# Hymba block in three-pass fp32r: PSUM pools by phase (single banks, double banks), and attention emitted in runs of two pairs

## The chip, the cores and the metric

One Trainium2 chip, one of its cores. The metric is the device time of one launch in microseconds. The kernel before takes 2512.08 us, the median of three runs (2510.38 to 2513.5).

## The reference

One decoder layer over x of 2048 tokens by 1024 channels, in float32:

```
hn    = rmsnorm(x, norm_mix_g)
x_lru, g_lru, q, k, v = split(hn @ w_in)          # 1024, 1024, 16x64, 2x64, 2x64
xc    = causal_conv4(x_lru)
r, i  = sigmoid(blockdiag(xc, w_a) + b_a), sigmoid(blockdiag(xc, w_x) + b_x)
a     = exp(-8 * r * softplus(-lam))
h_t   = a_t * h_(t-1) + sqrt(1 - a_t^2) * (i_t * xc_t)      # scan over tokens
y_lru = h * gelu(g_lru)
y_att = sliding window attention (window 128, learned sinks, 16 q heads, 2 kv heads)
x     = x + concat(rmsnorm(y_lru), rmsnorm(y_att)) @ w_out
x     = x + square(relu(rmsnorm(x) @ w_up)) @ w_down
out   = rmsnorm(x, norm_final_g)
```

The second mixer's norm needs the sum of squares of y_lru over all 1024 channels of a token, so it is complete only when the last block of channels is through the scan.

## The kernel before, in words

The 2048 tokens go through in two chunks of 1024 (`c` = 0, 1). Every fp32 product is three matmul passes in fp32r, hi·hi, hi·lo and lo·hi: ScalarE copies the operand to `hi` (L178 for weights), VectorE subtracts to get `lo` (L179).

A chunk has these stages. Stage 1 loads x, norms it (L208) and transposes it on TensorE (`tps`, L218), with the splits behind at L222 to L224. Then come the k and v projections (`kps`, `vps`, opened by `new_kv`, products at L236, L237, L239). The attention loop walks slots `s` = 0 to 16: in slot s, for four pairs `p` of query blocks, it emits `scores(p)` of head s (`sc`, L610), `values` of two older pairs (`av`, L664), `probs(p)` of head s-1 (two transposes `tp`, L640, read by ACT at L643 and DVE at L644 into `pf`), and one `piece`, six matmuls of a projection for later (`qps`, then `xps`, `gpps`). Every second slot ends a projection of q, whose splits `qs` stand at L588 and L589. Two heads of y are transposed by `flip` (`ytp`, L683). The LRU loop follows over eight channel blocks j: projections, convolution (L719), gates (`gps`, L879 to L881), the scan (L892), y (L896), its square (L900) and the sum `accq` (L901; for the last block on POOL). `token_rstd(accq)` transposes that sum (`sqt`, L701) to get the norm `r_lr`. Then W_out: matmuls `ops` (L960), added into x by DVE (L965), first the attention half of the rows (with `r_at`, known since attention's end), then the LRU half (with `r_lr`). The MLP's first half, `Up.run`, runs 16 pairs of hidden blocks, each of seven half-width products of a Strassen scheme (84 matmuls at L410) into `pa`, `pb` and the two halves of one tile `qr`; the DVE additions into `hid` stand at L440, L443 and L448. In its last pair chunk 0 starts stage 1 of chunk 1. The second half of the MLP (`dd`, L1187) runs after both chunks, with PSUM of its own.

What sets the order: the code is emitted in the order above, and a list scheduler of the framework then reorders it for each engine by what is ready, subject to the buffers; on the chip each engine's queue runs in that fixed order. A tile of PSUM can be given out when the last reader of its tag is through. PSUM before is laid out once for all stages but the last: two tiles of two banks (`mm0`, `mm1`) and four single ones (`b01` with two buffers, `b2`, `b3`):

```
    mmp = ps_stack.enter_context(tc.tile_pool(name="mmp", bufs=1, space=PSUM))
    hbp = ps_stack.enter_context(tc.tile_pool(name="hbp", bufs=1, space=PSUM))
```

`sqt` takes `b2` and `b3`; `ops` rotates through `mm0`, `mm1` and `b01`, so the two don't share a bank. In the attention `tp` is one bank with two halves, used by turns: pair p+2 waits until pair p's half was read.

Of the kernel before, what the change touches and what calls it, by code (L numbers as in the profile page):

```python
# [8 lines left out]
F32 = mybir.dt.float32  # L9
# [7 lines left out]
PSUM = bass.MemoryType.PSUM  # L17

P = 128
SEQ = 2048  # L20
D = 1024
# [4 lines left out]
HALF = 512  # L26
# [11 lines left out]
def hybrid_block_kernel(  # L38
# [40 lines left out]
    const = ctx.enter_context(tc.tile_pool(name="const", bufs=1))  # L79
    small = ctx.enter_context(tc.tile_pool(name="small", bufs=4))  # L80
    slots = ctx.enter_context(tc.tile_pool(name="slots", bufs=1))
    ps_stack = ExitStack()
    mmp = ps_stack.enter_context(tc.tile_pool(name="mmp", bufs=1, space=PSUM))
    hbp = ps_stack.enter_context(tc.tile_pool(name="hbp", bufs=1, space=PSUM))

# [21 lines left out]


    def bank(i, name, shape=(P, HALF)):
        if i < 2:
            return hbp.tile(list(shape), F32, name=name, tag="b01", bufs=2)
        return hbp.tile(list(shape), F32, name=name, tag=f"b{i}")

    def pair(i, name):

# [2 lines left out]
    mm_next = [0]  # L120

    def mm(name, i=None):

        if i is None:
            i = mm_next[0]
            mm_next[0] ^= 1
        return mmp.tile([P, D], F32, name=name, tag=f"mm{i}")

    def mm_halves(name, i=None):
        ps = mm(name, i)  # L130
        return [ps[:, :HALF], ps[:, HALF:]]

# [166 lines left out]
    class Up:  # L299
# [117 lines left out]
        def pair(self, fp):  # L417

            pa, pb = bank(fp % 2 * 2, "pa"), bank(fp % 2 * 2 + 1, "pb")
            qr = mm("qr", fp % 2)  # L420
            pq, pr = qr[:, :HALF], qr[:, HALF:]
            lo, hi = slice(0, HALF), slice(HALF, D)
            sc = U((11, 15)[fp % 2], "sc", F32, (P, 2, HALF))
            self.prod(pa, fp, "A11", "B11", True)
            act.activation(sc[:, 0], pa, AF.Copy)
            yield
            self.prod(pb, fp, "A12", "B21", True)
            c1 = self.hidden()
            dve.tensor_tensor(c1[:, lo], pb, sc[:, 0], op=ALU.add)
            yield  # L430
            self.prod(pa, fp, "S2", "T2", False)
            act.activation(sc[:, 1], pa, AF.Copy)
            yield
            self.prod(pq, fp, "A22", "T4", True)
            yield
            self.prod(pa, fp, "S3", "T3", False)
            s3 = small.tile([P, HALF], F32, name="s3", tag="s3", bufs=1)
            act.activation(s3, pa, AF.Copy)
            c2 = self.hidden()
            dve.tensor_tensor(c2[:, lo], pq, s3, op=ALU.add)  # L440
            yield
            self.prod(pr, fp, "S1", "T1", True)
            dve.tensor_tensor(c2[:, hi], pr, s3, op=ALU.add)  # L443
            act.activation(c2, c2, AF.Relu)
            act.activation(c2, c2, AF.Square)
            yield
            self.prod(pr, fp, "S4", "B22", False)
            dve.tensor_tensor(c1[:, hi], pr, sc[:, 1], op=ALU.add)  # L448
            act.activation(c1, c1, AF.Relu)
            act.activation(c1, c1, AF.Square)  # L450
            a12 = U(13, "a12", F32, (P, 2, HALF))
            a4 = U(14, "a4", F32, (P, HALF))
            dve.tensor_tensor(a12[:, 0], c1[:, hi], c2[:, hi], op=ALU.add)
            dve.tensor_tensor(a12[:, 1], a12[:, 0], c1[:, lo], op=ALU.subtract)
            dve.tensor_tensor(c1[:, hi], c1[:, lo], c1[:, hi], op=ALU.subtract)
            dve.tensor_tensor(a4, c2[:, lo], a12[:, 1], op=ALU.subtract)
            g, r = divmod(fp, 2)
            for o, y in enumerate((c1[:, lo], c2[:, hi], a12[:, 1], c2[:, lo], c1[:, hi], a4, a12[:, 0])):
                nc.sync.dma_start(actd[self.c][g][:, :, o, r * 2 * P:(r + 1) * 2 * P],
                                  y.rearrange("p (s n) -> p s n", s=2))  # L460
            yield
# [32 lines left out]
            self.next = (hn, steps) if steps else (None, None)  # L494

    def new_kv():
        k = mm("kps", 1)
        return k, ((k[:, :HALF], k[:, HALF:]), pair(0, "vps"))

# [10 lines left out]
    for c in range(NCH):  # L510
# [83 lines left out]
        class Head:  # L594
# [38 lines left out]
                dve.tensor_scalar(self.ls, self.ls, PSCALE, None, op0=ALU.mult)  # L633
                dve.reciprocal(self.ls, self.ls)

            def probs(self, p):

                tp = tpb[:, p % 2]
                for i in range(2):
                    pe.transpose(tp[:, i, :], self.st[:, 2 * p + i, :], ident)  # L640
                pf = U((20, 21, 12, 14)[pf_next[0] % 4], "pf", F16, (P, 3, 2, 2, P))
                pf_next[0] += 1
                act.activation(pf[:, 0, 0], tp, AF.Copy, scale=PSCALE)  # L643
                dve.scalar_tensor_tensor(out=pf[:, 0, 1], in0=tp, scalar=PSCALE, in1=pf[:, 0, 0],  # L644
                                         op0=ALU.mult, op1=ALU.subtract)

                nc.gpsimd.affine_select(out=pf[:, 1], in_=pf[:, 0], compare_op=ALU.is_gt, fill=0.0, base=0,  # L647
                                        pattern=[[0, 4], [-1, P]], channel_multiplier=1)
                nc.gpsimd.affine_select(out=pf[:, 2], in_=pf[:, 0], compare_op=ALU.is_ge, fill=0.0, base=0,
                                        pattern=[[0, 4], [1, P]], channel_multiplier=-1)  # L650
                self.pf[p] = pf
# [129 lines left out]
        lru_in = None  # L781
        for s in range(NH + 1):
            j = s // 2
            if s < NH:
                if s % 2 == 0:
                    yqs[j] = U(3 + j % 2, "yq", F32, (P, NT, P))
                heads[s] = Head(s, qs[j][s % 2], yqs[j])
            if s % 2 == 1:
                if j + 2 < KT:
                    piece, done = new_q(j + 2)  # L790
                else:
                    piece, done = (new_x if j + 2 == KT else new_gate)(0)
            for p in range(4):
                if s < NH:
                    heads[s].scores(p)
                    if p == 3:
                        heads[s].sums()
                if len(late) == 4:
                    for _ in range(2):
                        heads[late[0][0]].values(late.pop(0)[1])  # L800
                if s > 0:
                    heads[s - 1].probs(p)
                    late.append((s - 1, p))
                    if p == 3 and s % 2 == 1 and s > 1:
                        flip(j - 1, yqs[j - 1])
                piece(p if s % 2 else 4 + p)
            if s % 2 == 0:
                if j + 1 < KT:
                    qs[j + 1] = done()
                elif j + 1 == KT:  # L810
                    lru_in = done()
                else:
                    lru_in.append(done())
# [109 lines left out]
                parts.append(whole(new_gate(j + 1)))  # L923

        r_lr = token_rstd(accq, "lr")


        x1 = []
# [161 lines left out]
            dn.split("T1")  # L1090

    up.run(ahead)
    ps_stack.close()
    ddp = ctx.enter_context(tc.tile_pool(name="ddp", bufs=4, space=PSUM, reuse_waits="tile"))
    g3 = load_g(g_fin)

# [182 lines left out]
```

## Time and profile before

| what | value |
|---|---|
| median of three runs | 2512.08 us |
| profiled execution | 2512.32 us |
| span of its instructions | 2510.6 us |
| PE busy | 2420.6 us, 96% of the span |
| DVE busy | 1766.3 us, 70% |
| ACT busy | 1254.5 us, 50% |
| POOL busy | 457.4 us, 18% |
| mean granted TensorE clock | 0.996 of full speed |

The profiled execution is 0.24 us above the median of the runs, and 1.72 us of it lie outside the span. Stages in the trace: attention of chunk 0 from 65 to 257 us, LRU to 429, W_out to 617, first half of the MLP to 934; chunk 1 the same with attention from 997 to 1187, LRU to 1360, W_out to 1548, the first half to 1878; the second half to the end. PE is the engine in question: its times here are starts of instructions, since its ends are modelled and run on under the next start.

### The profile page before, as it was taken

How to read it: one execution, taken by the hardware profiler on the slowest of the kernel's cores; microseconds unless marked ns; L12 is line 12 of the kernel's file. 1: busy time of each engine (PE TensorE's matmuls, PEld its weight loads, DVE VectorE, ACT ScalarE, POOL GpSimd, SP SyncE). 2: the span in 40 equal slices, each digit the busy share in tenths (PEclk: the TensorE clock that was granted, in tenths of full speed). 3: DMA queues.
4: the chain of work that ended last, by engine and by line, in shares of the span. 5: the costliest groups of instructions: out<-in, count | busy, mean ns of one | idle time of the engine just before them, and what ended most of it. 6: DMA issues, size and time to landing. Idle time of an engine off the chain costs nothing.

```text
span 2510.6 us, 32534 instructions
## 1 busy us (share of the span) xinstructions
PE 2420.6 (96%) x12338; PEld 1974.2 (79%) x12338; DVE 1766.3 (70%) x2400; ACT 1254.5 (50%) x2084; POOL 457.4 (18%) x455
## 2 busy tenths in 40 slices
PE   7999999999999998999999998999999999999998
PEld 6877787787788877887778787788878877888886
DVE  6887566756655565886667847655564898887889
ACT  6666777414455455666778315444554233322335
POOL 0445000001333210454000001322310110111100
PEclk9999999999999999999999999999999999999999
DMA  4111113312344443111113312344464454443334
GB/s 161 37 52 52 45 46 107 115 51 100 118 142 155 157 155 130 43 52 51 46 45 124 111 42 101 133 145 146 148 212 129 154 163 147 142 138 122 125 98 164
DMA packets 132812, 276.37 MB, mean 110 GB/s; under 512 B 11184, under 2 KB 70576, under 8 KB 132656
## 3 DMA queue, kind: packets, MB, share of 16 engines
q1 hardware_dynamic: 124880, 246.50, 29.4%
q0 software_dynamic: 5184, 18.88, 2.0%
q10 hardware_dynamic: 2592, 8.91, 0.9%
q8 instruction: 97, 1.59, 0.3%
q14 instruction: 59, 0.48, 0.1%
HBM read 190.37 MB, written 83.89 MB: 109 GB/s over the span
## 4 chain that ended last, share of the span: by engine, by line
PE 66%; DVE 15%; issue 9%; ACT 7%; DMA 2%; POOL 1%; POOLq 0%; SPq 0%; ACTq 0%; DVEq 0%
PE dd L1187 14%; PE ops L960 10%; PE qr L410 10%; PE pa L410 9%; PE pb L410 3%; PE sc L610 2%; PE qps L239 2%; PE qps L236 2%; PE qps L237 2%; DVE xc L719 2%; DVE acc L1196 1%; PE xps L237 1%; PE xps L236 1%; PE xps L239 1%; DVE wlo L179 1%
## 5 line engine op out<-in xcount | busy, mean ns | idle before, releaser
L1196 DVE TENSOR_TENSOR acc<-dd,acc 128x1024 f32<-128x1024 f32 x211 | 255.4, 1219 | 85.1 <-PE dd L1187 84.6
L960 PE MATMUL ops<-whi,ht 128*128 128x512 f32 x1024 | 278.4, 391 | 1.0 <-DVE x L965 1.0
L990 ACT ACTIVATE ah<-araw 128x1024 fp32r<-128x1024 f32 x96 | 101.9, 1062 | 293.0 <-PE dd L1187 286.6
L960 PEld LDWEIGHTS ops<-whi,ht 128*128 128x128 f32 x1024 | 192.2, 188 | 42.7 <-DVE x L965 2.5
L960 PE MATMUL ops<-wlo,ht 128*128 128x512 f32 x512 | 159.7, 391 | 0.6 <-DVE wlo L179 0.5
L388 POOL TENSOR_TENSOR s<-wraw 128x512 f32<-128x512 f32 x32 | 43.0, 1343 | 593.2 <-issue 321.0
L178 ACT ACTIVATE whi<-wraw 128x1024 fp32r<-128x1024 f32 x84 | 88.5, 1054 | 120.7 <-PE ops L960 86.2
L647 POOL TENSOR_SCALAR_AFFINE_SELECT pf<-pf 128x512 f16<-128x512 f16 x128 | 87.3, 682 | 333.4 <-DVE pf L644 327.0
L991 DVE TENSOR_TENSOR al<-araw,ah 128x1024 fp32r<-128x1024 f32 x96 | 123.4, 1287 | 11.0 <-ACT ah L990 10.9
L624 ACT ACTIVATE st<-sc,mx 128x128 f32<-128x128 f32 x256 | 91.6, 364 | 60.1 <-DVE mx L621 59.6
L179 DVE TENSOR_TENSOR wlo<-wraw,whi 128x1024 fp32r<-128x1024 f32 x84 | 106.5, 1274 | 20.0 <-ACT whi L178 9.5
L960 PEld LDWEIGHTS ops<-wlo,ht 128*128 128x128 f32 x512 | 95.5, 188 | 21.4 <-DVE wlo L179 2.3
L236 PE MATMUL qps<-ht,whi 128*128 128x512 f32 x256 | 107.8, 421 | 0.0
L396 ACT ACTIVATE f2h<-wraw 128x1024 fp32r<-128x1024 f32 x32 | 33.9, 1061 | 142.6 <-DMA act<-hid 111.9
L237 PE MATMUL qps<-ht,whi 128*128 128x512 f32 x256 | 101.7, 397 | 0.0
L236 PE MATMUL xps<-ht,whi 128*128 128x512 f32 x256 | 101.5, 397 | 0.0
L239 PE MATMUL qps<-ht,wlo 128*128 128x512 f32 x256 | 101.3, 396 | 0.0
L237 PE MATMUL xps<-ht,whi 128*128 128x512 f32 x256 | 101.0, 394 | 0.0
L236 PE MATMUL gpps<-ht,whi 128*128 128x512 f32 x256 | 100.8, 394 | 0.0
L410 PE MATMUL qr<-hm,s 128*128 128x512 f32 x384 | 97.6, 403 | 2.7 <-DVE hid L443 2.7
L237 PE MATMUL gpps<-ht,whi 128*128 128x512 f32 x256 | 100.1, 391 | 0.0
L397 DVE TENSOR_TENSOR f2l<-wraw,f2h 128x1024 fp32r<-128x1024 f32 x32 | 39.1, 1223 | 79.1 <-ACT f2h L396 79.1
(327 smaller groups left out, 6852.5 us busy)
## 6 DMA issues: line engine op xcount, KB each, us to landing
araw<-act SPq DMA_DIRECT2D x96, 512.0 KB, 3.5
wraw<-in_w_up_dram SPq DMA_DIRECT2D x64, 512.0 KB, 3.2
act<-hid SPq DMA_DIRECT2D x128, 256.0 KB, 2.6
wraw<-in_w_in_dram SPq DMA_DIRECT2D x52, 512.0 KB, 3.2
act<-a SPq DMA_DIRECT2D x96, 256.0 KB, 2.6
wraw<-in_w_out_dram SPq DMA_DIRECT2D x32, 512.0 KB, 3.2
braw<-in_w_down_dram SPq DMA_DIRECT2D x28, 512.0 KB, 4.3
xt<-in_x_dram SPq DMA_DIRECT2D x16, 512.0 KB, 4.6
```

The lines of the kernel that those rows point to most:

```text
L178: act.activation(hi, raw, AF.Copy)
L179: (eng or dve).tensor_tensor(lo, raw, f32(hi), op=ALU.subtract)
L236: pe.matmul(ps[m], w[0][:, k * P:(k + 1) * P], hk(ht[m][0], k), start=(k == 0), stop=False)
L237: pe.matmul(ps[m], w[0][:, k * P:(k + 1) * P], hk(ht[m][1], k), start=False, stop=False)
L239: pe.matmul(ps[m], w[1][:, k * P:(k + 1) * P], hk(ht[m][0], k), start=False, stop=(k == KT - 1))
L410: pe.matmul(ps, w[a_][:, ks], hk(h[b_], k), start=first and k == 0 and i == 0, stop=k == KT // 2 - 1 and i == 2, skip_group_check=True)
L624: ins = act.activation(self.st[:, b, :], cur[:, i, :], AF.Exp, bias=self.mx[:, b:b + 1], accum_out=self.ls[:, b:b + 1])
L960: pe.matmul(ps[m], a_, wk[k][b_][:, hs], start=(k == 0 and a_ is yh and b_ == 0), stop=(k == kn - 1 and a_ is ylo))
L990: act.activation(hi, raw, AF.Copy)
L991: dve.tensor_tensor(lo, raw, f32(hi), op=ALU.subtract)
L1187: pe.matmul(o[:, i, :], a_[:, t0:t0 + P], b_[:, r, :], start=first and r == 0 and k == 0, stop=r == 1 and k == 2, skip_group_check=True)
L1196: dve.tensor_tensor(accs[blk][d_], o, accs[blk][d_], op=ALU.add)
```

## The change

Three things. First, `psum(*names)` closes the open pools of PSUM and opens others. A phase "sbp" has eight single banks `s0` to `s7`; it is open at the start (stage 1), and again from behind `r_lr` on: for W_out, the MLP's first half and the next chunk's stage 1. `new_kv` opens the old layout (`doubles()`) for projections, attention and LRU. Second, the tile `qr` of the MLP's first half becomes two tiles of a bank each, `pq` and `pr`; `mm_halves` gives two tiles where "sbp" is open. Third, the attention loop emits two pairs at a time: two `scores`, two `values`, two `probs`, two `piece`s. The odd pair of `probs` writes its transposes into `free`, half of an `mm` tile that no projection uses just then, the even one into `tpb`.

```diff
-    ps_stack = ExitStack()
-    mmp = ps_stack.enter_context(tc.tile_pool(name="mmp", bufs=1, space=PSUM))
-    hbp = ps_stack.enter_context(tc.tile_pool(name="hbp", bufs=1, space=PSUM))
+    phase = [None, {}]
+    def psum(*names):
+        if phase[0]:
+            phase[0].close()
+        phase[:] = [ExitStack(), {}]
+        for name in names:
+            phase[1][name] = phase[0].enter_context(
+                tc.tile_pool(name=name, bufs=1, space=PSUM, reuse_waits="tile"))
+    def doubles():
+        psum("mmp", "hbp")
+    psum("sbp")
...
     def bank(i, name, shape=(P, HALF)):
+        if "sbp" in phase[1]:
+            return half(4 + i, name)
...
+    def half(i, name):
+        return phase[1]["sbp"].tile([P, HALF], F32, name=name, tag=f"s{i}")
...
     def mm_halves(name, i=None):
+        if "sbp" in phase[1]:
+            if i is None:
+                i = mm_next[0]
+                mm_next[0] ^= 1
+            return [half(2 * i, name), half(2 * i + 1, name)]
...
-            qr = mm("qr", fp % 2)
-            pq, pr = qr[:, :HALF], qr[:, HALF:]
+            pq, pr = half(fp % 2 * 2, "pq"), half(fp % 2 * 2 + 1, "pr")
...
     def new_kv():
+        doubles()
...
-            def probs(self, p):
-                tp = tpb[:, p % 2]
+            def probs(self, p, free):
+                if p % 2 and free:
+                    tp = free[p // 2][:, :2 * P].rearrange("p (a n) -> p a n", a=2)
+                else:
+                    tp = tpb[:, p // 2]
...
+            free = mm_halves("tp", (s + 1) // 2 % 2) if 0 < s < NH - 1 else None
...
-            for p in range(4):
+            for p0 in (0, 2):
                 if s < NH:
-                    heads[s].scores(p)
-                    if p == 3:
+                    for p in (p0, p0 + 1):
+                        heads[s].scores(p)
+                    if p0:
                         heads[s].sums()
...
-                    heads[s - 1].probs(p)
-                    late.append((s - 1, p))
-                    if p == 3 and s % 2 == 1 and s > 1:
+                    for p in (p0, p0 + 1):
+                        heads[s - 1].probs(p, free)
+                        late.append((s - 1, p))
+                    if p0 and s % 2 == 1 and s > 1:
                         flip(j - 1, yqs[j - 1])
-                piece(p if s % 2 else 4 + p)
+                for p in (p0, p0 + 1):
+                    piece(p if s % 2 else 4 + p)
...
         r_lr = token_rstd(accq, "lr")
+        psum("sbp")
```

Line numbers move with it: L236, L237, L239 become L258, L259, L261; L410 is L432, L443 is L464, L589 is L611, L610 is L632, L644 is L669, L640 is L665, L701 is L726, L879 to L881 are L910 to L912, L901 is L932, L960 is L992.

How the queues move is shown at three places. The first is PE at the end of the LRU of chunk 0 (`sqt` transposes the sum `accq`, `gps` are the last gates, `ops` W_out's matmuls). Before:

```order
L960 MATMUL ops<-whi,ht 128x512 x4
L960 MATMUL ops<-wlo,ht 128x512 x2
L960 MATMUL ops<-whi,ht 128x512 x4
L960 MATMUL ops<-wlo,ht 128x512 x2
L960 MATMUL ops<-whi,ht 128x512 x2
L960 MATMUL ops<-whi,ht 128x512 [waits DVE_49] x2
L701 MATMUL sqt<-ident,accq 128x128 [waits Pool_49]
L701 MATMUL sqt<-ident,accq 128x128 x3
L701 MATMUL sqt<-ident,accq 128x128 [waits Activation_49]
L701 MATMUL sqt<-ident,accq 128x128 x3
```

After the change:

```order
L911 MATMUL gps<-xlo,gd 128x512
L912 MATMUL gps<-xhi,gd 128x512
L910 MATMUL gps<-xhi,gd 128x512 [waits Activation_49]
L911 MATMUL gps<-xlo,gd 128x512
L912 MATMUL gps<-xhi,gd 128x512
L726 MATMUL sqt<-ident,accq 128x128 [waits Pool_49]
L726 MATMUL sqt<-ident,accq 128x128 x3
L726 MATMUL sqt<-ident,accq 128x128 [waits Activation_49]
L726 MATMUL sqt<-ident,accq 128x128 x3
L992 MATMUL ops<-whi,ht 128x512 [waits PE_49]
L992 MATMUL ops<-whi,ht 128x512
L992 MATMUL ops<-wlo,ht 128x512 x2
```

Before, 110 matmuls `ops` of W_out stand between the last `gpps` and the first `sqt`, with the last 12 `gps` among them; now the 12 `gps` alone stand there, and every `ops` stands behind `sqt`. In chunk 1 it is the same, also by 110. The wait for POOL at the first `sqt` is the same.

The second place is PE in a pair of the MLP's first half (`qr`, now `pq` and `pr`; the second and third products of a pair that write one half of it). Before:

```order
L410 MATMUL pb<-hm,a1h 128x512
L410 MATMUL qr<-hm,s12h 128x512 [waits DVE_49]
L410 MATMUL qr<-hm,s12h 128x512
L410 MATMUL qr<-hm,s12l 128x512
L410 MATMUL qr<-hm,s12h 128x512 x2
L410 MATMUL qr<-hm,s12l 128x512
...
L410 MATMUL pb<-hm,a1l 128x512
L410 MATMUL pb<-hm,a1h 128x512 x2
L410 MATMUL qr<-hm,s_6085 128x512 [waits DVE_49]
L410 MATMUL qr<-hm,s_6085 128x512 x11
L410 MATMUL pb<-hm,a1l 128x512
```

After:

```order
L432 MATMUL pa<-hm,f2h 128x512 x2
L432 MATMUL pa<-hm,f2l 128x512
L432 MATMUL pr<-hm,s12h 128x512 [waits PE_49]
L432 MATMUL pr<-hm,s12h 128x512
L432 MATMUL pr<-hm,s12l 128x512
L432 MATMUL pr<-hm,s12h 128x512 x2
...
L432 MATMUL pa<-hm,a1l 128x512
L432 MATMUL pb<-hm,a1h 128x512
L432 MATMUL pr<-hm,s_6140 128x512 [waits DVE_49]
L432 MATMUL pr<-hm,s_6140 128x512 x11
L432 MATMUL pb<-hm,a1h 128x512
```

Before, both runs on `qr`, the one on `s12h` and the one on `s`, wait for DVE; now the run on `s12h` waits for nothing but PE's own earlier work, and the run on `s` still waits for DVE.

The third place is DVE in a slot of attention in which a q is finished (`qs`, the split of the new q; `pf`, the read of transposed probabilities). Before:

```order
L620 TENSOR_REDUCE mx<-sc 128x2
L589 SCALAR_TENSOR_TENSOR qs<-qps,qs 64x1024
L621 TENSOR_SCALAR mx<-mx,snk 128x2
L644 SCALAR_TENSOR_TENSOR pf<-tp,pf 128x256
L618 COPY_PREDICATED sc<-prevm,sc 128x2x128
L620 TENSOR_REDUCE mx<-sc 128x2
L589 SCALAR_TENSOR_TENSOR qs<-qps,qs 64x1024
L621 TENSOR_SCALAR mx<-mx,snk 128x2
L644 SCALAR_TENSOR_TENSOR pf<-tp,pf 128x256
L618 COPY_PREDICATED sc<-prevm,sc 128x2x128
```

After:

```order
L669 SCALAR_TENSOR_TENSOR pf<-tp,pf 128x256
L656 RECIPROCAL ls<-ls 128x8
L201 TENSOR_TENSOR wlo<-wraw,whi 128x1024
L637 COPY_PREDICATED sc<-prevm,negt 128x128
L611 SCALAR_TENSOR_TENSOR qs<-qps,qs 64x1024
L638 COPY_PREDICATED sc<-prevm,sc 128x128
L640 COPY_PREDICATED sc<-prevm,sc 128x2x128
L642 TENSOR_REDUCE mx<-sc 128x2 x2
L611 SCALAR_TENSOR_TENSOR qs<-qps,qs 64x1024
L643 TENSOR_SCALAR mx<-mx,snk 128x2 x2
L669 SCALAR_TENSOR_TENSOR pf<-tp,pf 128x256
```

Before, a `pf` stands between the two `qs`; now both `qs`, two reads of maxima and the weight split `wlo` stand between one `pf` and the next.

## Rows read from the trace of the kernel before

**Rows 1.** The page of the whole run: busy time, share and instructions of each engine.

```profile
PE 2420.6 (96%) x12338; PEld 1974.2 (79%) x12338; DVE 1766.3 (70%) x2400; ACT 1254.5 (50%) x2084; POOL 457.4 (18%) x455
```

**Rows 2.** What PE waited for: us in total, times, longest us.

```profile
PE tp L640 <- DVE pf L644: 13.2, 16, 1.1
...
PE pa L410 <- ACT hm L348: 7.1, 2, 3.5
...
PE qr L410 <- DVE hid L440: 5.5, 4, 4.2
...
PE sqt L701 <- POOL accq L901: 2.7, 2, 1.7
PE qr L410 <- DVE hid L443: 2.7, 2, 1.9
```

**Rows 3.** PE groups from 429.4 to 459.3 us; columns as in the page's part 5.

```profile
L960 PE MATMUL ops<-whi,ht 128*128 128x512 f32 x74 | 21.0, 393 | 0.3 <-DVE x L965 0.3
L960 PE MATMUL ops<-wlo,ht 128*128 128x512 f32 x36 | 11.4, 390 | 0.0
...
L701 PE MATMUL sqt<-ident,accq 128*128 128x128 f32 x1 | 0.3, 327 | 1.0 <-POOL accq L901 1.0
```

**Rows 4.** The timeline of all engines from 441 to 460 us, chunk 0's tail.

```profile
447.62 1.40 DVE L965 SCALAR_TENSOR_TENSOR x<-ops,rs_at,x 128x512 f32<-128x512 f32 x2
...
451.50 2.35 DVE L892 TENSOR_TENSOR_SCAN r<-a,hcar,i 128x1024 f32<-128x1024 f32 x1
...
455.72 1.06 ACT L900 ACTIVATE r<-yl 128x1024 f32<-128x1024 f32 x1 [1.86 <-DVE yl L896]
...
456.86 2.36 POOL L901 TENSOR_TENSOR accq<-accq,r 128x1024 f32<-128x1024 f32 x1 [1.65 <-ACT r L900]
```

**Rows 5.** Busy time by stretch, LRU's end and W_out, chunk 0; busy (count), PEclk, DMA share, GB/s.

```profile
429.40:459.30 29.90, 28.58 (x124) 22.54 (x122) 25.60 (x31) 24.25 (x32) 4.51 (x5) 1.00 0.61 205
...
459.30:610.00 150.70, 149.35 (x675) 122.65 (x676) 93.40 (x128) 41.55 (x65) 8.15 (x6) 1.00 0.19 68
```

**Rows 6.** Busy time by stretch behind a wait, the first half's start.

```profile
631.00:635.00 4.00, 3.68 (x10) 2.96 (x10) 4.00 (x5) 4.00 (x6) 2.49 (x2) 0.57 0.07 25
```

**Rows 7.** The timeline from 149.9 us, attention of chunk 0.

```profile
150.10 0.48 PE L236 MATMUL qps<-ht,whi 128*128 128x512 f32 x1
150.41 0.40 PE L237 MATMUL qps<-ht,whi 128*128 128x512 f32 x1
150.65 0.40 PE L239 MATMUL qps<-ht,wlo 128*128 128x512 f32 x1
```

**Rows 8.** The same timeline from 158.5 to 166.1 us, one slot's end.

```profile
161.84 1.22 DVE L589 SCALAR_TENSOR_TENSOR qs<-qps,qs 64x1024 fp32r<-64x1024 f32 x1
...
163.71 0.44 PE L640 MATMUL tp<-ident,st 128*128 128x128 f32 x2 [0.83 <-DVE pf L644]
```

**Rows 9.** Busy time by stretch, a period of two slots.

```profile
148.74:170.88 22.14, 21.25 (x202) 18.05 (x200) 18.08 (x47) 14.37 (x48) 11.34 (x18) 1.00 0.14 50
```

**Rows 10.** PE's timeline from 684 to 708 us, one pair of the first half.

```profile
686.76 0.39 PE L410 MATMUL pb<-hm,a1h 128*128 128x512 f32 x1
...
689.89 0.39 PE L410 MATMUL pb<-hm,a1h 128*128 128x512 f32 x1
...
690.35 0.61 PE L410 MATMUL pb<-hm,a1h 128*128 128x512 f32 x2
...
693.73 0.39 PE L410 MATMUL pb<-hm,a1l 128*128 128x512 f32 x1
...
703.48 0.62 PE L410 MATMUL pa<-hm,a1h 128*128 128x512 f32 x2
...
706.20 0.39 PE L410 MATMUL pb<-hm,a1h 128*128 128x512 f32 x1
```

**Rows 11.** Busy time by stretch, chunk 0's end to chunk 1's start.

```profile
934.00:967.00 33.00, 26.87 (x144) 21.19 (x143) 27.13 (x40) 25.16 (x44) 0.00 (x0) 1.00 0.75 255
```

**Rows 12.** PE's timeline where the first half ends in chunk 1.

```profile
1870.24 1.19 PE L410 MATMUL qr<-hm,s12h 128*128 128x512 f32 x2 [4.18 <-DVE hid L440]
```

More of the change, by code (lines that the diff above doesn't have):

```diff
@@ L111, in bank @@
     def bank(i, name, shape=(P, HALF)):
+        if "sbp" in phase[1]:
+            return half(4 + i, name)
         if i < 2:
-            return hbp.tile(list(shape), F32, name=name, tag="b01", bufs=2)
-        return hbp.tile(list(shape), F32, name=name, tag=f"b{i}")
+            return phase[1]["hbp"].tile(list(shape), F32, name=name, tag="b01", bufs=2)
+        return phase[1]["hbp"].tile(list(shape), F32, name=name, tag=f"b{i}")
+    def half(i, name):
+        return phase[1]["sbp"].tile([P, HALF], F32, name=name, tag=f"s{i}")
     def pair(i, name):
@@ L126, in mm @@
             mm_next[0] ^= 1
-        return mmp.tile([P, D], F32, name=name, tag=f"mm{i}")
+        return phase[1]["mmp"].tile([P, D], F32, name=name, tag=f"mm{i}")
     def mm_halves(name, i=None):
+        if "sbp" in phase[1]:
[3 more added lines that the diff above has]
+            return [half(2 * i, name), half(2 * i + 1, name)]
         ps = mm(name, i)
@@ L1092, in hybrid_block_kernel @@
     up.run(ahead)
-    ps_stack.close()
+    phase[0].close()
     ddp = ctx.enter_context(tc.tile_pool(name="ddp", bufs=4, space=PSUM, reuse_waits="tile"))
```

## The prediction

> **What bounds the kernel now.** I read the page first, then what PE waited for, then PE's work stage by stage, and last the timeline at the places where the change moves rows. PE is busy for 96% of the span [rows 1]; no other engine is above 70%. What PE waits for is a short list of small waits [rows 2]: the transposes of attention for DVE's read of the bank (13.2 us in 16 waits), the first half's start for ACT (7.1 in 2), the first half's products for DVE's sums (5.5 and 2.7), and the second mixer's sum of squares for POOL (2.7 in 2). So a change gains at most what these lists hold, but loses every microsecond for which PE is left without work. The place to look at is therefore not where PE waits most, but where the new order takes work away from in front of a wait.
>
> **The tail of the LRU, the largest term.** From PE's last projection of the LRU to the transposes `sqt` there are 29.9 us [rows 5], and PE is busy for 28.58 of them. What fills it: 110 matmuls `ops` [rows 3] and 12 `gps`. Meanwhile the last channel block runs through its chain: gates, scan on DVE at 451.50, square on ACT at 455.72, sum on POOL at 456.86 for 2.36 us, that is until 459.22 [rows 4]; `sqt` then waits only 1.0 us for it [rows 3]. The order of the changed kernel keeps that chain on ACT, DVE and POOL but puts all 110 `ops` behind `sqt`, since the new pools open only after the last tile of the old ones, which is `sqt`. Queues run in order, so PE has 12 `gps` and then nothing until POOL is done. A matmul of this size takes (706.20 - 703.48) / 12 = 0.2267 us [rows 10]; 110 of them take 24.94 us. Behind `sqt`, W_out keeps PE busy for 149.35 of 150.70 us [rows 5], so nothing there takes the 24.94 us back. Two chunks: **+49.9 us**. Can the chain end sooner with an empty PE? DVE no longer has `x` sums there, but the last of these before the scan ends at 447.62 + 1.40 [rows 4], before DVE has to wait for ACT; I give that nothing, and at most their 1.4 us in each chunk.
>
> **The clock behind that hole.** Behind a wait of PE at the first half's start (3.5 us, for ACT [rows 2]) the granted clock is 0.57 on average over 4 us [rows 6], its lower level, 1.2 GHz, for most of that time. PE loses 4 x (1 - 0.57) = 1.7 us there. The new holes are about 27 us long, so I take the same price for each: **+3.4 us**. Bounds: nothing, if the wait before the rows is not the cause, and twice that.
>
> **Attention.** A period of two slots takes 22.14 us, of which PE is busy 21.25 and DVE 18.08 [rows 9]. In each period one transpose waits 0.83 us for DVE's read, behind a split `qs` of 1.22 us [rows 8]. Runs of two pairs halve the number of switches between kinds of work: a first projection matmul behind another kind takes 150.41 - 150.10 = 0.31 us, one inside a run 150.65 - 150.41 = 0.24 [rows 7], so four runs of projections less per period save 4 x 0.07 = 0.3 us. At best the wait goes too: -1.1 us a period. At worst the new DVE order, where both `qs` stand ahead of the next read of transposes, lengthens that wait by one `qs`, 1.22 us, less the 0.3: +0.9. There are 7.5 periods in a chunk, 15 in all: -17 to +14. Neither row is nearer than the other, since a second bank helps three of the four transposes and the double `qs` hurts the fourth; I take the middle, **-2 us**.
>
> **The MLP's first half.** In a pair, one matmul on `pb` and the 12 on `s12h` take 689.89 - 686.76 = 3.13 us, against 13 x 0.2267 = 2.95; two on `pb` and the 12 on `s` take 693.73 - 690.35 = 3.38, against 3.17 [rows 10]. So each of the two runs that wait for DVE costs 0.18 to 0.21 us. The order shows that the run on `s12h` no longer waits for DVE and the run on `s` still does. 28 pairs lie in the steady part: 28 x 0.18 = **-5 us**. Bounds: nothing, if what costs is the change of bank itself, and 28 x 0.39 = -11 if both go. A rule bears on this: the Trainium skill, "Perfetto Trace Analysis", section "Optimizing Tensor Performance", says that independent groups of matmuls should rotate through different PSUM banks so that reading one out lies under the next group's work. By it the separate tiles would take both costs away, -11 us for this term and 6 us off the sum; the order still has a wait on one run, so I follow the order.
>
> **Smaller places.** At the chunk's border PE is busy 26.87 of 33.00 us [rows 11]; 12 `kps` matmuls that ran between the transposes now wait for the last split of the transposes, because the banks change hands there: up to 12 x 0.2267 = 2.7 us more, less what separate banks save the splits: **+2** (0 to +6, the idle time doubled). At the first half's end the `s12h` run waits 4.18 us for DVE [rows 12]; this wait goes, but the next run waits for later work of the same engine: **-2** (0 to -4). The rest of stage 1, W_out's banks and the start I cost at nothing: what they save lies under PE's own work in these stages.
>
> **Sum.** Against the profiled execution, 2512.3 us, which is 0.2 above the median of the runs: 2512.3 + 49.9 + 3.4 - 2 - 5 + 2 - 2 = **2558.6 us**, some 46 slower.
>
> **The rivals.**
> *Banks were what held attention and the first half.* With more banks `tp` never waits for a read of its own bank: its 13.2 us [rows 2] vanish, with 15 x 0.3 = 4.5 for the switches and 11 in the first half. 2512.3 + 53.3 - 17.7 - 11 + 2 - 2 = 2537. The page named above says the same in general (the Trainium skill, "Perfetto Trace Analysis", "Optimization Strategy"): a gap that repeats on the engine that should be full can mean too little PSUM for the next tile. For it: 16 waits at the same place. Against it: DVE is busy 18.08 of 22.14 us there, and its order puts more, not less, ahead of the read. Chance 0.13.
> *Attention stalls on DVE.* The free half that the odd pair writes belongs to the q just finished, so `tp` waits for the second `qs` itself, and `sc` queues behind it. That gives the +14 of the bound in place of -2: 2575. For it: the order above. Against it: the wait is one per period, and PE's runs ahead of it are twice as long. Chance 0.15.
> *Faster.* The chain to POOL ends much sooner once PE no longer delays the gates, so that the hole closes. Even with the best of all other terms (-17 - 11 - 4, no clock loss, nothing at the border) the tails have to stay below 32 - 5 = 27 us together, 13.5 a chunk, to fall below the bound: the chain must shrink by more than 11 us. Then some 2505. Against it: from the scan at 451.50 to 459.22 alone [rows 4] scan, y, square and sum fill 7.7 us in turn on three engines, and what is ahead of them waits on ACT's own queue rather than on PE. Chance 0.03.
> *The change doesn't do what it says.* The hole is as forecast for a part only, because ready work is found for it or one chunk's chain is early: between 2507 and 2532, with the bound of no change at the lower end. Chance 0.05, of which 0.02 within 0.2%.
> My forecast, 2558.6 with the bounds of its unknown terms, has the remaining 0.64.
>
> **How the numbers follow.** 0.2% of the time, 5 us, is about what a measurement of this kernel can tell from no change. The range runs from the first rival, with a little of its width, to the second: 2535 to 2575; about 0.2 is left out, below it mostly the faster and the partial cases, above it a stall in attention with a dearer border. Faster 0.03, the same 0.02, slower 0.95.
>
> **What would show it.** In the profile after, PE should wait some 26 to 27 us, twice, at `sqt` for POOL's `accq`, be the largest wait on the list, and W_out should be longer by 25 us behind it; for some microseconds after each hole the granted clock should be near half. The pair of the first half should take 19.25 us in place of 19.45, with its run on `pr` behind `pa` in 2.72 us. In attention a period should lie between 21.0 and 23.0 us, and the waits of `tp` say which bound was right. If `sqt` waits under 15 us, the first step is wrong; if a period is over 23 us, the third is.

## The result, and the profile after

The changed kernel takes 2570.98 us (median of four runs, 2568.57 to 2574.69) against 2511.23 for the kernel before: a ratio of 1.0239 with a 95% interval of 1.0221 to 1.0257. It is some 60 us slower. The forecast was 2558.6, the range 2535 to 2575.

The page of the changed kernel, whole run (busy time, share, instructions), answers to [rows 1]:

```profile
PE 2432.9 (95%) x12338; PEld 1989.7 (77%) x12338; DVE 1740.5 (68%) x2400; ACT 1256.1 (49%) x2084; POOL 444.0 (17%) x455
```

What PE waited for in the changed kernel (us in total, times, longest), answers to [rows 2]:

```profile
PE sqt L726 <- POOL accq L932: 44.2, 2, 22.5
PE tps L240 <- DVE xt L230: 9.6, 5, 3.5
PE tp L665 <- DVE qs L611: 8.3, 6, 2.5
...
PE pr L432 <- DVE hid L464: 7.2, 4, 2.2
...
PE kps L258 <- DVE ht L246: 3.1, 1, 3.1
...
PE tp L665 <- DVE pf L669: 1.4, 3, 0.8
```

One wait has grown to the head of the list: `sqt` for POOL's sum, 44.2 us in two, where it was 2.7. The wait of `tp` for `pf` has all but gone (13.2 to 1.4 us); a wait for `qs` has come in its place. The hole, as busy time by stretch (the columns of [rows 5]), and PE's groups in it:

```profile
435.30:465.40 30.10, 3.99 (x13) 1.94 (x12) 22.59 (x27) 23.35 (x31) 4.83 (x5) 0.65 0.60 208
466.50:610.00 143.50, 143.50 (x626) 118.91 (x627) 75.87 (x103) 24.53 (x33) 2.05 (x3) 0.98 0.15 50
```

```profile
L910 PE MATMUL gps<-xhi,gd 128*128 128x512 f32 x4 | 1.7, 473 | 4.0 <-ACT r L913 2.3 <-ACT xhi L751 1.6
L911 PE MATMUL gps<-xlo,gd 128*128 128x512 f32 x4 | 1.7, 423 | 0.7 <-DVE xlo L752 0.7
L912 PE MATMUL gps<-xhi,gd 128*128 128x512 f32 x4 | 1.6, 390 | 0.0
```

Where 124 instructions of PE filled 28.58 us [rows 5], 13 fill 3.99. W_out behind it leaves PE no idle time at all. Before, 1.35 us of it were idle (150.70 - 149.35, [rows 5]); nothing more than that can be made up. The chain that it waits for, in the timeline (start, duration, engine, line, idle time before and releaser), answers to [rows 4]:

```profile
457.36 2.35 DVE L923 TENSOR_TENSOR_SCAN r<-a,hcar,i 128x1024 f32<-128x1024 f32 x1
...
461.58 1.06 ACT L931 ACTIVATE r<-yl 128x1024 f32<-128x1024 f32 x1 [2.96 <-DVE yl L927]
462.72 3.69 POOL L932 TENSOR_TENSOR accq<-accq,r 128x1024 f32<-128x1024 f32 x1 [1.65 <-ACT r L931]
...
466.46 1.97 PE L726 MATMUL sqt<-ident,accq 128*128 128x128 f32 x8 [22.54 <-POOL accq L932]
```

The chain is the same and no shorter: POOL's sum is 1.33 us longer than before (3.69 against 2.36 us, [rows 4]). To place the 60 us, here is PE's time between marks: the starts on PE of the first scores, the first `sqt` of each sum, the last `gpps`, the first matmul on `pa`, the first `tps` of chunk 1, the first `dd`, and the last row on PE. Span against span the difference is 2571.5 - 2510.6 = 60.9 us.

| stretch | before, us | after, us | difference |
|---|---|---|---|
| start to first scores | 64.9 | 68.2 | +3.3 |
| attention, chunk 0 and 1 | 191.9, 189.0 | 194.6, 185.6 | +2.7, -3.4 |
| LRU to its last `gpps`, both | 172.3, 173.1 | 172.3, 172.2 | 0.0, -0.9 |
| tail (`gpps` to `sqt`) and W_out, both | 188.3, 186.5 | 214.7, 213.9 | +26.4, +27.4 |
| first half of chunk 0, to `tps` of chunk 1 | 316.8 | 315.6 | -1.3 |
| border, `tps` to first scores of chunk 1 | 63.5 | 72.9 | +9.4 |
| first half of chunk 1, to `dd` | 332.2 | 328.9 | -3.3 |
| second half | 620.3 | 620.9 | +0.6 |

The tails and W_out are 53.8 of the 60.9 us; the border is the next.

### The profile page after: what moved, and what is told of

The parts are those of the page before. It is cut to its first block, busy times and chain, and to the rows that moved or that the text cites. A ratio compares the mean times of both kernels' runs of the same rounds, so it can differ in the third digit from the quotient of the medians.

```text
span 2571.5 us, 32634 instructions
## 1 busy us (share of the span) xinstructions
PE 2432.9 (95%) x12338; PEld 1989.7 (77%) x12338; DVE 1740.5 (68%) x2400; ACT 1256.1 (49%) x2084; POOL 444.0 (17%) x455
## 4 chain that ended last, share of the span: by engine, by line
PE 66%; DVE 16%; issue 8%; ACT 7%; POOL 1%; DMA 1%; POOLq 0%; SPq 0%; ACTq 0%; DVEq 0%
PE dd L1219 14%; PE ops L992 14%; PE pa L432 9%; PE pr L432 7%; PE pq L432 3%; PE pb L432 3%; DVE xc L744 2%; PE sc L632 1%; DVE acc L1228 1%; PE xps L259 1%; PE xps L258 1%; PE xps L261 1%; DVE wlo L201 1%; DVE qs L611 1%; DVE r L923 1%
## 5 line engine op out<-in xcount | busy, mean ns | idle before, releaser
L992 PE MATMUL ops<-whi,ht 128*128 128x512 f32 x1024 | 278.2, 392 | 0.0
L992 PEld LDWEIGHTS ops<-whi,ht 128*128 128x128 f32 x1024 | 192.9, 189 | 40.0
L992 PE MATMUL ops<-wlo,ht 128*128 128x512 f32 x512 | 159.2, 392 | 0.0
L672 POOL TENSOR_SCALAR_AFFINE_SELECT pf<-pf 128x512 f16<-128x512 f16 x128 | 96.2, 751 | 336.4 <-DVE pf L669 332.1
L410 POOL TENSOR_TENSOR s<-wraw 128x512 f32<-128x512 f32 x32 | 42.2, 1318 | 554.0 <-DMA wraw<-in_w_up_dram 236.5
L646 ACT ACTIVATE st<-sc,mx 128x128 f32<-128x128 f32 x256 | 91.1, 366 | 46.3 <-DVE mx L643 40.5
L992 PEld LDWEIGHTS ops<-wlo,ht 128*128 128x128 f32 x512 | 96.5, 189 | 20.3 <-DVE wlo L201 0.3
L997 DVE SCALAR_TENSOR_TENSOR x<-ops,rs_at,x 128x512 f32<-128x512 f32 x96 | 67.6, 746 | 62.6 <-PE ops L992 57.1
L432 PE MATMUL pr<-hm,s 128*128 128x512 f32 x384 | 99.8, 410 | 7.2 <-DVE hid L464 7.2
L258 PE MATMUL qps<-ht,whi 128*128 128x512 f32 x256 | 105.2, 411 | 0.1
L258 PE MATMUL xps<-ht,whi 128*128 128x512 f32 x256 | 101.1, 395 | 0.0
L261 PE MATMUL qps<-ht,wlo 128*128 128x512 f32 x256 | 100.9, 394 | 0.0
L259 PE MATMUL qps<-ht,whi 128*128 128x512 f32 x256 | 100.8, 394 | 0.0
L259 PE MATMUL xps<-ht,whi 128*128 128x512 f32 x256 | 100.7, 393 | 0.0
L258 PE MATMUL gpps<-ht,whi 128*128 128x512 f32 x256 | 100.5, 393 | 0.0
```

The costliest lines, as they stand in the source:

```text
L258: pe.matmul(ps[m], w[0][:, k * P:(k + 1) * P], hk(ht[m][0], k), start=(k == 0), stop=False)
L259: pe.matmul(ps[m], w[0][:, k * P:(k + 1) * P], hk(ht[m][1], k), start=False, stop=False)
L261: pe.matmul(ps[m], w[1][:, k * P:(k + 1) * P], hk(ht[m][0], k), start=False, stop=(k == KT - 1))
L432: pe.matmul(ps, w[a_][:, ks], hk(h[b_], k), start=first and k == 0 and i == 0, stop=k == KT // 2 - 1 and i == 2, skip_group_check=True)
L646: ins = act.activation(self.st[:, b, :], cur[:, i, :], AF.Exp, bias=self.mx[:, b:b + 1], accum_out=self.ls[:, b:b + 1])
L992: pe.matmul(ps[m], a_, wk[k][b_][:, hs], start=(k == 0 and a_ is yh and b_ == 0), stop=(k == kn - 1 and a_ is ylo))
```

## The experiments

**sqt in the singles.** The pools are closed one line earlier, so that `sqt` takes two of the single banks.

```diff
-        r_lr = token_rstd(accq, "lr")
-        psum("sbp")
+        psum("sbp")
+        r_lr = token_rstd(accq, "lr")
...
                 tp = bank(2 + hf, "sqt", (P, 4, P))
+                if "sbp" in phase[1]:
+                    tp = tp.rearrange("p (a n) -> p a n", a=4)
```

> The changed kernel with the singles opened ahead of r_lr, so that sqt lies in two of them and W_out's matmuls may go ahead of it in PE's queue. Theory (the order of PE's queue makes the hole at sqt, some 52 us of the 60): 2516 to 2522 us, the wait of sqt for POOL's accq back at 1 to 2 us a chunk, the rest of the kernel as in the changed one. Rival (the pools by phase cost by themselves, the hole is only where it shows): 2545 us or more, and a hole elsewhere in the same stretch.

Measured: 2526.8 us, 1.0056 of the kernel before (1.0042 to 1.0069). PE's waits and its groups from 435 to 465.3 us:

```profile
PE sqt L728 <- POOL accq L934: 6.1, 2, 4.4
```

```profile
L994 PE MATMUL ops<-whi,ht 128*128 128x512 f32 x50 | 13.5, 389 | 0.0
L994 PE MATMUL ops<-wlo,ht 128*128 128x512 f32 x25 | 7.8, 389 | 0.0
...
L912 PE MATMUL gps<-xhi,gd 128*128 128x512 f32 x4 | 2.0, 546 | 2.6 <-ACT xhi L753 1.6 <-ACT r L915 1.0
```

The kernel before took 2513.21 us in the same measurement, so 13.6 us of the 60 remain: one line gives back 46. That falls short of the 2516 to 2522 I expected, and is far below the rival's 2545. The longer of the two waits at `sqt` is 4.4 us, not the 1 to 2 expected. 75 `ops` stand ahead of `sqt` now, not the 110 of the kernel before. Before, 26 `ops` stood ahead of the last `gps` in PE's queue; now none does, so none passes the last tiles of the closed pools, and PE idles while these `gps` wait for ACT and DVE. The other 35 are 35 x 0.2267 = 7.9 us a chunk, and W_out is 7.2 and 7.6 us longer than before. So the wait at `sqt` was the big case of something that shows at the `gps` too: work of a new pool did not go ahead of the last tiles of a closed one.

**ops behind sqt.** The kernel before, its pools untouched, with a dependency by hand for the scheduler:

```diff
+                    last_sqt[0] = pe.transpose(tp[:, b, :], ...
...
+                                ins = pe.matmul(ps[m], a_, wk[k][b_][:, hs],
...
+                                if grp == 0 and k0 == 0:
+                                    after(ins, last_sqt[0])
```

> The kernel before, with PSUM as it was, and W_out's first group of matmuls ordered behind the transposes sqt by hand. Theory (order alone is enough): 110 matmuls a chunk move, 2 x (24.9 + 1.7) = 53 us more, 2562 to 2567 us, with a wait of 20 to 27 us at sqt in each chunk and a lower clock behind it. Rival (pools matter): under 2530 us.

Measured: 2567.8 us, 1.0219 (1.0205 to 1.0233), +54.6 us. PE's waits, and the busy time of the hole and of the stretch behind it:

```profile
PE sqt L703 <- POOL accq L903: 44.3, 2, 22.2
```

```profile
428.50:459.50 31.00, 4.08 (x13) 1.94 (x12) 23.62 (x27) 23.95 (x32) 5.83 (x5) 0.64 0.64 208
459.50:464.00 4.50, 4.46 (x15) 3.88 (x16) 3.04 (x6) 0.72 (x2) 1.11 (x2) 0.50 0.76 249
```

The order alone, without any change to the banks, makes the same wait (44.3 against 44.2 us) and nearly the whole loss. With the run before it, the step holds both ways: the order put in makes the loss, the order taken out ends most of it.

**Attention alone.** The kernel before with the changed attention loop and `probs`, as in the diff of the change.

> The kernel before with the attention of the changed one alone: runs of two pairs, transposes of odd pairs in an idle half. The trace of the changed kernel has attention 3.1 us longer in chunk 0 and 3.0 us shorter in chunk 1. Theory (attention is its own matter, the sum near nothing): within 4 us of the kernel before. Rival (runs of two pairs pay when nothing else is changed): 5 us or more faster. Second rival (DVE's order makes it dearer): 5 us or more slower.

Measured: 2509.61 us, 0.9989 (0.9980 to 0.9997), 3.6 us faster. Attention takes 195.0 us in chunk 0 and 185.6 in chunk 1, as in the changed kernel. The theory holds, at its edge: attention explains nothing of the 60 us. Its two chunks sum to -0.3 us, so the 3.6 do not come from attention's own stretches; where they come from was not followed.

**Joined halves.** On the run with `sqt` in the singles, the first four single banks are two tiles of two banks again.

```diff
-            pq, pr = half(fp % 2 * 2, "pq"), half(fp % 2 * 2 + 1, "pr")
+            qr = wide(fp % 2, "qr")
+            pq, pr = qr[:, :HALF], qr[:, HALF:]
...
-            return [half(2 * i, name), half(2 * i + 1, name)]
+            ps = wide(i, name)
+            return [ps[:, :HALF], ps[:, HALF:]]
...
+    def wide(i, name):
+        return phase[1]["sbp"].tile([P, D], F32, name=name, tag=f"w{i}")
```

> As the run with sqt in the singles, but each two of the four first singles are one tile of two banks again, so that the two halves of a product tile, of stage 1's and of W_out's tiles are given out and waited for together. Theory (separate halves pay 0.18 us in each of 28 pairs): 5 us slower than the run with sqt in the singles, with 19.45 us a pair in place of 19.25. Rival (two waits a pair go): 11 us slower. Second rival (what costs is the change of bank, not the shared tile): no difference.

Measured: 2530.67 us, 3.9 more than the run it builds on (2527.92 to 2530.93 against 2525.14 to 2528.78). The two first halves are 1.6 and 4.6 us longer (317.2 and 332.0 against 315.6 and 327.4), as in the kernel before; the start is 3.5 us shorter. A steady pair takes 19.43 us here and 19.23 in the run it builds on, as the theory has it. So separate halves are worth about 6 us in the first halves and cost 3.5 at the start; the second rival falls, the first too.

**Singles opened late.** `psum("sbp")` moves from behind `r_lr` to behind W_out.

```diff
         r_lr = token_rstd(accq, "lr")
-        psum("sbp")
...
+        psum("sbp")
         if c + 1 < NCH:
             up.run()
```

> The changed kernel with the singles opened behind W_out instead of behind r_lr, so that LRU, sqt and W_out share the old layout. Theory (closing the pools is a border that no work crosses; the run with sqt in the singles kept 75 of the 110 matmuls ahead of sqt and W_out was still 7.3 and 7.6 us longer in its two chunks): W_out as in the kernel before, 158 and 156 us, and 2510 to 2518 us. Rival (each border costs its 7 us wherever it lies): W_out short, but the first half of the MLP 7 us longer in each chunk, 2524 us or more.

Measured: 2539.72 us, 1.0106 (1.0092 to 1.0120). The rival holds. PE's waits:

```profile
PE pa L432 <- DVE hm L246: 25.7, 2, 12.8
PE tps L240 <- DVE hm L246: 10.6, 2, 5.3
```

All 110 `ops` are ahead of `sqt` again, but the wait has moved to the next border: the first `pa` waits 12.8 us in each chunk. In the kernel before it did not wait, as it stood ahead of the last transposes `tps` of W_out's tokens, and only the second product waited, 3.5 us for ACT [rows 2]; here it stands behind all of them. From `sqt` to the end of the first half chunk 0 takes 482.4 us against 475.0 and chunk 1 496.6 against 488.5, so this border costs 7.5 and 8.1 us, less what the separate halves gain there; that is the rival's 7. The rest of the excess is mostly the chunks' border (73.0 us against 63.5) and the start (67.6 against 64.9), which the rival had left out. The pools of the change are opened with `reuse_waits="tile"`, the old ones without it. Here the old layout has it too and all 110 `ops` are ahead of `sqt`, so it is not this parameter that held them back.

**Singles in the pairs only.** As the last, with the start and chunk 0's last pair in the old layout.

```diff
-    psum("sbp")
+    doubles()
...
-            pq, pr = half(fp % 2 * 2, "pq"), half(fp % 2 * 2 + 1, "pr")
+            if "sbp" in phase[1]:
+                pq, pr = half(fp % 2 * 2, "pq"), half(fp % 2 * 2 + 1, "pr")
+            else:
+                pq, pr = mm_halves("qr", fp % 2)
...
     def new_kv():
-        doubles()
+        if "mmp" not in phase[1]:
+            doubles()
...
             for fp in range(2, NF // 2):
+                if fp + 1 == NF // 2 and c + 1 < NCH:
+                    doubles()
```

> As the run with the singles opened late, but the start (stage 1 of chunk 0) and chunk 0's last pair with stage 1 of chunk 1 in the old layout too; singles are open for the other pairs alone. Theory (the borders at the start and between the chunks cost 3 us and 4 to 9 us): 6 to 12 us faster than the run with the singles opened late, 2500 to 2508 us, stage 1 of chunk 1 to its first scores 63 to 65 us. Rival (the new border before the last pair costs as much as the one it takes away): 3 us faster, the start alone.

Measured: 2523.83 us, 1.0042 (1.0029 to 1.0054), 15.9 less than the run with the singles late, more than expected; the level expected was missed because that run lay higher. The border of the chunks falls from 73.0 to 62.4 us (63.5 before), the start from 67.6 to 64.0. That shows the forecast's small term to have been a large one: the border between stage 1 and the projections costs up to 10 us, and goes with the border of the pools. Its price varies, though: with the same code and the same order of PE there it took 67.1 us in the run with `sqt` in the singles, and in runs that close no pool there it lay between 62.4 and 66.2 us. The traces say where the 5.8 us between 72.9 and 67.1 are. In the changed kernel PE is busy for 13.0 us of that stretch at the lower clock, in the other run for 5.8 (rows below, and in the part on the border); at half rate that makes 3.6 us, and PE idles 2.3 us less. Why the clock fell for a shorter time stays open.

```profile
967.60:974.40 6.80, 5.78 (x21) 4.88 (x21) 6.79 (x10) 5.73 (x8) 0.00 (x0) 0.50 0.60 205
```

**Idle half in even slots.** On that run.

```diff
-            free = mm_halves("tp", (s + 1) // 2 % 2) if 0 < s < NH - 1 else None
+            free = mm_halves("tp", (s + 1) // 2 % 2) if s % 2 == 0 and 0 < s < NH - 1 else None
...
-                    tp = tpb[:, p // 2]
+                    tp = tpb[:, p // 2 if free else p % 2]
```

> As the run with singles in the pairs only, but the odd pair's transposes go to the idle half only in even slots; in odd slots, where that half belongs to the q that was just finished, they take turns in one bank as before. Theory (in the changed kernel's chunk 0 tp waits 8.3 us in 6 waits for the second qs, none in chunk 1): 3 to 7 us faster, attention of chunk 0 from 195 down to 187 to 191 us. Rival (in odd slots the old wait for pf comes back at 0.8 us each): no difference in chunk 0 and chunk 1 dearer, 3 us slower at most.

Measured: 2532.52 us, 8.7 more than the run it builds on; attention is 198.2 and 186.7 us. PE's waits:

```profile
PE tp L671 <- DVE pf L675: 13.0, 15, 2.6
```

My theory fell: the wait for `qs` goes, and the old one for `pf` comes back longer (10.7 us in chunk 0, where it was 6.9 before the change). The rival is nearer, but its 3 us at most are too few. Of the 7.8 us between the two profiled spans (2523.0 and 2530.8) attention holds 4.4; the rest is spread over other stretches, and I did not follow it.

**Runs without the idle half.** The kernel before, attention in runs of two pairs, `tp = tpb[:, p % 2]` as before.

> The kernel before with attention in runs of two pairs, but no transposes in the idle half: they take turns in one bank as before. Theory (the gain of the run with the whole attention, 3.6 us, is fewer switches; the idle half helps in one chunk and hurts in the other): 2 to 6 us faster than the kernel before. Rival (the idle half makes the gain, two runs in one bank wait for DVE's read): as the kernel before or slower, with the wait of tp for pf above its 13 us.

Measured: 2511.88 us, 0.9997 (0.9988 to 1.0006): no difference from the kernel before, attention 196.2 and 186.2 us. So it is the runs of two that cost 4 us in chunk 0 and give 3 in chunk 1; against this run, the idle half adds 1.2 us of gain in chunk 0 and 0.6 in chunk 1. Neither theory has it quite: there is no gain, and `tp` waits 10.3 us for `pf`, not above 13.

**Halves in two tiles.** The kernel before, one edit.

```diff
-            qr = mm("qr", fp % 2)
-            pq, pr = qr[:, :HALF], qr[:, HALF:]
+            pq, pr = mm("pq", 0)[:, :HALF], mm("pr", 1)[:, :HALF]
```

> The kernel before with one edit in the MLP's first half: pq takes half of the tile mm0 and pr half of mm1, in every pair, so that the run on s12h no longer shares a tile with the half that DVE is reading; no pool is closed anywhere. Theory (the gain of the separate halves is the shared tile's wait, and the borders of the pools alone eat it): 4 to 6 us faster than the kernel before, 2507 to 2510 us, the two stretches of the first half some 1.5 and 4 us shorter. Rival (the gain needs all eight banks single, because a tile per half leaves one buffer where there were two): no difference.

Measured: 2503.7 us, 0.9968 (0.9956 to 0.9980), 8.3 faster, more than the 4 to 6 expected. The first halves take 313.3 and 325.1 us (316.8 and 332.2 before); the border of the chunks takes 2 more. The timeline of PE in this kernel, two successive pairs:

```profile
685.51 3.02 PE L410 MATMUL pr<-hm,s 128*128 128x512 f32 x12
...
704.72 1.66 PE L410 MATMUL pr<-hm,s 128*128 128x512 f32 x6
```

That is 19.21 us from pair to pair; the next takes 19.25, and they go on by turns, against 19.43 in a steady pair of the kernel before. One buffer for each half is enough, and no pool has to be closed for it.

**Two tiles, runs in chunk 1.** That, with attention in runs of two pairs (and the idle half) in chunk 1 alone:

```diff
+            free = mm_halves("tp", (s + 1) // 2 % 2) if c and 0 < s < NH - 1 else None
...
+            runs = ((0, 1), (2, 3)) if c else ((0,), (1,), (2,), (3,))
+            for ps_ in runs:
```

> As the run with the halves in two tiles, and attention in runs of two pairs with the idle half in chunk 1 alone, chunk 0 as in the kernel before. Theory (the runs are worth 3.4 us in chunk 1 and cost 3.0 in chunk 0): 3 us faster than the run with the halves in two tiles, 2503 to 2507 us, attention 192 us in chunk 0 and 185.5 in chunk 1. Rival (what chunk 1 gains was bought in chunk 0, as work done earlier there): no difference, attention of chunk 1 at 188 to 189 us.

Measured: 2499.26 us, 0.9949 (0.9936 to 0.9961), attention 192.0 and 185.6 us: 4.4 faster than the run it builds on, with attention as the theory has it. It beats both kernels, by 12.7 and some 72 us, and keeps most of what the change gained without its borders.

## Why the prediction was right, step by step

**The tail: right.** The prediction gave 49.9 + 3.4 = 53.3 us to the moved `ops` and the clock; tails and W_out measured 53.8. That the two come so close is in part luck, as small terms cancel: POOL's longer sum made each tail some 1.2 us longer, the clock behind the holes cost 4.5 us and not 3.4 (below), W_out's 1.35 us of idle time went, and some 1.5 us less were not followed. The wait at `sqt` is 22.5 us in chunk 0 and not 26 to 27, as part of the hole lies in front of the gates (4.0 + 0.7 us in the groups above); the stretch from `gpps` to `sqt` stays near the 30.2 us of before, at 31.4. What settled the step was the order of PE's queue read against the trace: how many matmuls stand in front of a wait, before and after.

**The clock: the mechanism right, its reach too small.** Behind the hole the granted clock is at its lower level (1.2 GHz) in the changed kernel, until 471.8 us:

```profile
466.46:471.80 5.34, 5.34 (x17) 4.57 (x18) 3.00 (x6) 0.35 (x2) 1.12 (x2) 0.50 0.68 239
471.80:610.00 138.20, 138.20 (x611) 114.39 (x610) 72.91 (x97) 24.22 (x31) 0.93 (x1) 1.00 0.13 43
...
1427.30:1430.90 3.60, 3.57 (x13) 3.19 (x14) 2.57 (x5) 0.59 (x2) 1.12 (x2) 0.50 0.73 255
```

PE is busy all that time, so half of it is lost: 0.50 x (5.34 + 3.57) = 4.5 us for both chunks, against the 3.4 I took. It is low inside the hole too (0.65 over it, above), but in chunk 0 only from 444.5 us on, when PE had nothing left to run. The prediction priced the clock nowhere else. The changed kernel also runs at the lower level in the first halves, where PE is busy for 18.4 us at it (10.0 before), at the chunks' border (below), and for 3.4 us each in the start and in attention's chunk 0.

**The border of the chunks: the term that was mis-sized.** "+2 (0 to +6, the idle time doubled)" measured +9.4. I had counted 12 `kps` that move behind the last split. In the trace of the kernel before 19 `kps` start ahead of the last of the transposes, 4.3 us of filling and not 2.7, and the trace of the changed kernel has more waits than that one:

```profile
980.26 4.62 PE L432 MATMUL pr<-hm,s 128*128 128x512 f32 x12 [2.21 <-DVE hid L464]
987.14 1.05 PE L240 MATMUL tps<-ident,xt 128*128 128x128 f32 x3 [2.26 <-DVE xt L230]
...
995.44 0.80 PE L258 MATMUL kps<-ht,whi 128*128 128x512 f32 x1 [3.11 <-DVE ht L246]
```

With no `kps` to fill in, PE waits several times in turn, and the clock falls: 12 matmuls on `pr` take 4.62 us, where in a steady pair they take 3.04 (below). The busy time of that stretch shows it, 0.79 of the clock over 40 us, at the lower level in two parts:

```profile
965.00:1005.00 40.00, 30.41 (x134) 23.77 (x133) 25.07 (x36) 22.79 (x38) 0.00 (x0) 0.79 0.62 217
...
980.40:983.80 3.40, 3.40 (x9) 2.63 (x10) 1.00 (x2) 3.40 (x6) 0.00 (x0) 0.50 0.87 323
987.20:1000.80 13.60, 9.62 (x29) 7.16 (x30) 9.32 (x14) 5.70 (x8) 0.00 (x0) 0.50 0.76 244
```

I priced the clock behind the long holes, and not here, where it is the larger part: 0.50 x (3.40 + 9.62) = 6.5 us by this estimate, and PE's idle time grew by 3.5 us (10.3 against 6.9). The start, which "I cost at nothing", was +3.3. Both went when the old layout stayed open there; but the start was short with joined halves too, where the pools still change, so it goes by the separate halves, not by the border; how it does stays open. These two missed amounts, 7.4 and 3.3 us, are most of the 14.6 between the 46.3 us forecast and the 60.9 between the spans.

The measured 2570.98 us lies nearer to the second rival's 2575 than to the forecast's 2558.6, but not by that rival's cause: attention cost nothing in sum, where the rival gave it 14 us.

**The first half: the pairs right, the sum smaller.** The run on `s12h` takes 2.72 us, as said, and a pair 19.23 (19.25 said), from these rows of PE's timeline in the changed kernel:

```profile
718.02 0.62 PE L432 MATMUL pr<-hm,s12h 128*128 128x512 f32 x2
...
720.74 0.62 PE L432 MATMUL pa<-hm,a1h 128*128 128x512 f32 x2
...
721.69 3.04 PE L432 MATMUL pr<-hm,s 128*128 128x512 f32 x12
...
740.92 3.04 PE L432 MATMUL pr<-hm,s 128*128 128x512 f32 x12
```

Pairs and the end of the first half gave -4.6 together, of -7 forecast. The lower clock took part of the gain back: the 8.4 us more that PE is busy at it there (18.4 against 10.0) cost some 4 us at half rate, an estimate. The rule of the Trainium skill on rotating banks ("Perfetto Trace Analysis", "Optimizing Tensor Performance") would have had -11 for the pairs. A steady pair gained 0.20 us of the 0.39 that this takes (19.23 against 19.43), and the run on `s` still waits, so the order was the better guide in this kernel. With the halves in two tiles the rule's direction holds, by 8.3 us for the whole kernel.

**Attention: the sum right, its parts not seen.** -0.7 measured, -2 forecast, from +2.7 in chunk 0 and -3.4 in chunk 1. From one flip (`ytp`) to the next, a period mostly takes 22.2 us in chunk 0 and 21.6 to 21.7 in chunk 1 (22.1 and 22.2 before), inside the 21.0 to 23.0 forecast. One period of chunk 0 is outside: 25.9 us, and 23.4 before. In chunk 0 the second rival's mechanism is there, `tp` held up by the second `qs`. The timeline shows it in its longest case, which lies in that period, and the clock is at its lower level from 147.5 to 150.9 us behind it:

```profile
146.48 1.23 DVE L611 SCALAR_TENSOR_TENSOR qs<-qps,qs 64x1024 fp32r<-64x1024 f32 x1
...
147.86 0.66 PE L665 MATMUL tp<-ident,st 128*128 128x128 f32 x2 [2.47 <-DVE qs L611]
```

In chunk 1 it is not, and neither is the old wait (6.3 us there before). The prediction took one period for both chunks, which turned out differently. Why chunk 0 loses stays open. The wait for `qs` is not shown to be the cause, since runs of two without the idle half, and so without that wait, lost 4 us there too.

## What to carry to other kernels

Closing a pool of PSUM and opening another was a border in the scheduler's order as well as in the memory: what uses the new pool stood behind the last tiles of the old one at the three kinds of place seen here (in front of `sqt` or behind it, between W_out and the first half, between stage 1 and the projections). It cost 7 to 27 us a time at the first place, 7 to 8 at the second and 4 to 10 at the third. That the price grows with the time that the last tile has to wait is a reading of these three places; no run varied it. So put such a border where the engine that sets the time has nothing to run ahead anyway, or, better, get the separate buffers within the pools that are open. Before trusting a list of waits, count what the order puts in front of each wait: the wait of 1 us at `sqt` hid 30 us of waiting that other work filled. And where a change opens idle time on PE, price the clock at every place where it does so, not at the longest hole alone.

## What the runs showed of the hardware

The last sum `accq` on POOL took 2.34 to 2.36 us in 18 of the 24 cases (two chunks in each of twelve kernels). It took 3.69 and 3.49 us in the changed kernel and in the run with `ops` behind `sqt`, and 3.02 in chunk 0 of the two runs with `sqt` in the singles. What differs is DVE's work beside it. Of the two sets of rows below, the first (the changed kernel) has the sum held up, the second (chunk 1 of the kernel before) DVE's `ht`:

```profile
461.46 1.41 DVE L939 SCALAR_TENSOR_TENSOR ht<-yre,vec,ht 128x512 fp32r<-128x512 f32 x2
462.72 3.69 POOL L932 TENSOR_TENSOR accq<-accq,r 128x1024 f32<-128x1024 f32 x1 [1.65 <-ACT r L931]
462.79 1.22 DVE L201 TENSOR_TENSOR wlo<-wraw,whi 128x1024 fp32r<-128x1024 f32 x1
```

```profile
1387.63 2.35 POOL L901 TENSOR_TENSOR accq<-accq,r 128x1024 f32<-128x1024 f32 x1 [1.65 <-ACT r L900]
1387.69 3.50 DVE L908 SCALAR_TENSOR_TENSOR ht<-yre,vec,ht 128x512 fp32r<-128x512 f32 x2
```

In the six long cases a split `wlo` of 1.22 us, or in the 3.02 an `ht` of 0.73, ran beside the sum in its usual time, and the sum was longer by 0.7 to 1.3 us. In the other 18 an `ht` beside the sum took 1.8 to 2.85 us, where it takes 0.74 alone; DVE's sums `x` ran beside it and held up neither. So with `wlo` and `ht` one of the two waited; what decides which one stays open.

At the chunks' border of the changed kernel the clock fell to 0.50 though no wait of PE there was longer than 3.1 us; PE was busy for 30.41 of the 40 us. In the kernel before it stayed at 1.00 there, with PE busy for 26.87 of 33.00 us [rows 11].
